# An encoder trunk whose weight chunks are split into a high and a low part by two DMA loads, in place of a load, a cast and a subtraction

## The chip, the cores and the metric

The kernel runs on one core of a Trainium2 chip. The metric is the device time of one execution in microseconds (us), median of several. The names of the engines in the profile: PE is TensorE (matmuls; PEld are its weight loads), DVE is VectorE, ACT is ScalarE, POOL is GpSimd, SP is SyncE, which here only issues DMAs (SPq is its queue).

## The reference

Two layers run over x, 512 tokens of width 1024, in float32. Each layer normalises x, projects it, runs two groups of heads (bidirectional retention and differential attention), adds their projection to x, and adds a gated feed-forward product:

```python
    for l in range(DEPTH):                      # DEPTH = 2
        h = rms_norm(x, attn_norm_g[l])
        proj = h @ w_in[l]
        rq, rk, rv, rg, dq, dk, dv = jnp.split(proj, split_at, axis=-1)
...
        ret = rms_norm(ret, ret_norm_g[l]) * jax.nn.silu(rg.reshape(shp))
...
        da = diff_attention(dqn, dkn, dv.reshape(B, S, DIFF_HEADS, DIFF_V_DIM), lam, slopes)
...
        x = x + jnp.concatenate([ret, da], axis=-1) @ w_out[l]

        h = rms_norm(x, ffn_norm_g[l])
        x = x + (jax.nn.silu(h @ w_gate[l]) * (h @ w_up[l])) @ w_down[l]
    return x
```

w_gate and w_up are 1024 x 2816 and w_down is 2816 x 1024, so more than half of the matmuls are in the feed-forward part.

## The kernel before

**Split products.** All weight products run on TensorE in the type fp32r, which keeps fewer bits than float32. To get float32's accuracy, each operand is split in two: a high part `hi`, the value rounded to fp32r, and a low part `lo`, the value minus `hi`. A product is then three matmuls, hi by hi, hi by lo and lo by hi (`mm3`, L173 to L176).

**Weight chunks.** Weights lie in HBM as chunks of 128 partitions by 1024 floats (512 KB; in the last pass over w_down 768 wide). `chunk` (L169) loads one into a tile `raw` (3 buffers) with a DMA that SP issues (L152), and splits it with `split_chunk`: ScalarE casts `raw` into `hi` (L166), and VectorE subtracts `hi` from `raw` into `lo` (L167). `hi` and `lo` have NHL = 3 buffers each. A full chunk feeds 24 matmuls of 512 columns (or as many operands of 256 columns for the value projections). There are 212 splits: 204 of chunks, and 8 half chunks at the start.

**Stages of a layer.** `project_first` (four weight chunks against all eight tiles of h), then values, gates and keys, the attention heads with further projections woven in between (`weave`), the retention pairs with the output projection woven in, the second norm, and the feed-forward part in three passes over 8, 8 and 6 tiles of the inner width (`FFN`): in each pass w_gate and w_up chunks in turn, then eight w_down chunks.

**The start.** In layer 0 the weights of `project_first` come as half chunks of 512 columns, `raw` and x by turns: for each of eight tiles x is loaded, split and scaled (`hi`, L185), squared (`sq`, L215) and summed. The constants `cst_sb` are loaded after all of it (L301). The eight short passes `wk` on ScalarE need them.

**What sets the order.** Code is written engine by engine through a framework that builds a graph, estimates each instruction's time and writes each engine's instructions in the order of that estimate. On the chip each engine, and the queue of DMAs that an engine issues, then works through its own list in order, and waits at an instruction until its semaphores are reached. Instructions of one engine do not overtake each other. Tiles come from pools: a new tile of a tag waits until the oldest buffer of the tag has been read for the last time.

Of the kernel before, what the change touches and what calls it, by code (L numbers as in the profile page):

```python
# [8 lines left out]
F32 = mybir.dt.float32  # L9
F32R = mybir.dt.float32r  # L10
AF = mybir.ActivationFunctionType
ALU = mybir.AluOpType

P = 128
# [21 lines left out]
PAIRS = [0, 0, 1, 0, 1, 2, 0, 1, 2, 3, 1, 2, 3, 2, 3, 3]  # L36


NW, NQK, NMIX, NAH, NHL = 12, 11, 20, 3, 3


PRM_AG, PRM_FG, PRM_RG, PRM_QG, PRM_KG, PRM_DG = 0, 16, 32, 34, 36, 38
# [9 lines left out]
def encoder_kernel(ctx: ExitStack, tc: tile.TileContext, xT, wfirst, wsingle, wvv, wout, wgu, wdn, prm, lam, cst, outT):  # L52
    nc = tc.nc
# [3 lines left out]
    wpool = ctx.enter_context(tc.tile_pool(name="wpool", bufs=3))  # L57
# [6 lines left out]
    def nm(s):  # L64
        uid[0] += 1
        return f"{s}{uid[0]}"

    def big(s, dt=F32, tag="w", bufs=NW):
        return tpool.tile([P, T], dt, tag=tag, name=nm(s), bufs=bufs)
# [19 lines left out]
    def f32(ap):  # L89
        return ap.bitcast(F32)  # L90
# [20 lines left out]
    xscr = ctx.enter_context(tc.tile_pool(name="dpool", bufs=1, space=bass.MemoryType.DRAM)).tile([KT, P, T], F32, name="xscr")  # L111

    def load_x(src, kt):
        xt = big("x", tag="qk", bufs=NQK)
        nc.sync.dma_start(xt, src[kt])
        return xt
# [26 lines left out]
    nc.vector.memset(eps_sb, EPS)  # L143


    def new_chunk(n, pieces=1):
        return wpool.tile([P, 1024], F32, tag="raw", name=nm("raw"), bufs=3), n, pieces

    def load_piece(new, src, i):
        raw, n, pieces = new  # L150
        s = slice(i * n // pieces, (i + 1) * n // pieces)
        nc.sync.dma_start(raw[:, s], src[:, s])  # L152

    def load_chunk(src, n=1024, pieces=1):
        new = new_chunk(n, pieces)
        for i in range(pieces):
            load_piece(new, src, i)
        return new

    def split_chunk(raw, n, pieces):  # L160
        hi = wpool.tile([P, 1024], F32R, tag="hi", name=nm("hi"), bufs=NHL)
        lo = wpool.tile([P, 1024], F32R, tag="lo", name=nm("lo"), bufs=NHL)
        q = n // pieces
        for i in range(pieces):
            s = slice(i * q, (i + 1) * q)
            nc.scalar.copy(hi[:, s], raw[:, s])  # L166
            nc.vector.tensor_tensor(lo[:, s], raw[:, s], f32(hi[:, s]), op=ALU.subtract)  # L167
        return hi, lo

    def chunk(*a, **kw):  # L170
        return split_chunk(*load_chunk(*a, **kw))

    def mm3(out, L, R, start, stop):  # L173
        nc.tensor.matmul(out, L[0], R[0], start=start, stop=False)  # L174
        nc.tensor.matmul(out, L[0], R[1], start=False, stop=False)  # L175
        nc.tensor.matmul(out, L[1], R[0], start=False, stop=stop)  # L176

    def cut(pair, *idx):
        return tuple(t[idx] for t in pair)

    def split_scaled(src, col, tag, bufs):

        hi = big("hi", F32R, tag, bufs)
        lo = big("lo", F32R, tag, bufs)
        nc.scalar.activation(hi, src, AF.Copy, scale=col)  # L185
        nc.vector.scalar_tensor_tensor(lo, src, col, f32(hi), op0=ALU.mult, op1=ALU.subtract)
        return hi, lo
# [88 lines left out]
        nc.vector.tensor_scalar(gk, prm_sb[:, PRM_KG : PRM_KG + DEPTH], -0.5, None, op0=ALU.mult)  # L276
        consts.update(gk=gk, lg=lg, lamn=lamn, gq=gq, gd=gd, wk=wk, rs=rs)

    def layer(l, n1, h, x_src, first_raw):


        def project_first():
            banks = [b() for b in (acc_bank, acc_bank, sc_bank, sc_bank)]
            for c in range(4):
                w = [t.rearrange("p (k f) -> p k f", f=512) for t in split_chunk(*first_raw[c])]
                for k in range(2):
                    kt = 2 * c + k
                    for i, ps in enumerate(banks):
                        mm3(ps, cut(w, slice(None), k, slice(i * P, (i + 1) * P)), h[kt], kt == 0, kt == KT - 1)
            return banks  # L290

        def project(name, m):
            w = [t.rearrange("p (k f) -> p k f", f=P) for t in chunk(wsingle[l, SINGLE.index((name, m))])]
            ps = acc_bank()
            for kt in range(KT):
                mm3(ps, cut(w, slice(None), kt), h[kt], kt == 0, kt == KT - 1)
            return ps

        first = project_first()
        if l == 0:  # L300
            nc.sync.dma_start(cst_sb, cst)  # L301
# [44 lines left out]
        def project_v(which, half, get=acc_bank):  # L346

            w = [[t.rearrange("p (k f) -> p k f", f=256) for t in chunk(wvv[l, which, half, i])] for i in range(2)]
            for i in range(4):
                ps = get()[:, :256]  # L350
                for kt in range(KT):
                    hh = cut(h[kt], slice(None), slice(i * P, (i + 1) * P))
                    mm3(ps, hh, cut(w[kt // 4], slice(None), kt % 4), kt == 0, kt == KT - 1)
                yield i, ps
# [190 lines left out]
        q, k = [None] * 4, [None] * 4  # L545
# [58 lines left out]
        def project_out(half, get, *then):  # L604
            parts = mix[4:] if half == 0 else mix[:4]
            for c in range(4):
                w = [t.rearrange("p (k f) -> p k f", f=256) for t in chunk(wout[l, half, c])]
                for m in (2 * c, 2 * c + 1):
                    if half == 0:
                        x.append(load_x(x_src, m))  # L610
                    ps = get()
                    for kt in range(4):
                        mm3(ps, cut(w, slice(None), kt, slice((m % 2) * P, (m % 2 + 1) * P)), parts[kt], kt == 0, kt == 3)
                    residual(m, x[m], ps, *then)
                    yield
# [13 lines left out]
        for a0, a1 in FFN:  # L629
            act = []  # L630
            for ff in range(a0, a1):
                pgu = []
                for gu in range(2):
                    w = [t.rearrange("p (k f) -> p k f", f=P) for t in chunk(wgu[l, ff, gu])]
# [12 lines left out]
            for m in range(KT):  # L647
                w = chunk(wdn[l, m][:, a0 * P : a1 * P], (a1 - a0) * P)
# [9 lines left out]
                        nc.sync.dma_start(outT[m], x[m])  # L658
        return n3, h3

    n, h, raws = Norm(), [], []
    for kt in range(KT):
        if kt % 2 == 0:
            raws.append(new_chunk(1024, 2))
        load_piece(raws[-1], wfirst[0, kt // 2], kt % 2)
        xt = load_x(xT, kt)
        h.append(split_scaled(xt, prm_sb[:, PRM_AG + kt : PRM_AG + kt + 1], "h", 16))
        n.add(xt)
    for l in range(DEPTH):
        if l:  # L670
            raws = [load_chunk(wfirst[l, c]) for c in range(4)]
        n, h = layer(l, n, h, xT if l == 0 else xscr, raws)


def _constants():
# [84 lines left out]
```

## Time and profile before

| | us |
|---|---|
| median of 3 runs | 1287.65 (1287.47 to 1289.41) |
| the profiled execution | 1287.41 |
| its span in the profile | 1285.6 |
| busy: TensorE, VectorE, ScalarE, GpSimd | 1271.1, 769.2, 570.5, 17.3 |
| load traffic | 93 GB/s mean |

How to read the profile's lines: a group has line, engine, operation, output tile <- input tiles, shapes and count, then busy us, mean ns of one, and the idle time of the engine ahead of it with what ended it. A timeline's line begins with start and duration in us. In a line of the waits stand the waiting engine, tile and line, the releaser, the total in us, the number and the longest. A table by stretches has the stretch, its length, busy us (and instructions) of PE, PEld, DVE, ACT and POOL, and then the granted TensorE clock, the DMA engines' busy share and GB/s. The matmuls' ends are modelled and overlap the next start, so the distance of starts says how fast TensorE goes.

The time of the profiled execution is 1.8 us longer than its span; the rest lies around it.

### The profile page before, as it was taken

The numbers are of one execution on the slowest core, as the hardware profiler recorded it, in microseconds if no ns is written. First come the engines' busy times: TensorE is split into PE (matmuls) and PEld (weight loads), VectorE is DVE, ScalarE is ACT, GpSimd is POOL, SyncE is SP. The second block draws the span as 40 slices with busy tenths as digits, with TensorE's granted clock in tenths as the row PEclk, the third lists the DMA queues.
The fourth block names the chain that finished last, engine by engine and source line by source line (L and its number), as shares of the span: only waits on it lengthen the run. The fifth ranks groups of instructions, "written<-read, shape, count | busy, mean of one in ns | idle before, by whom it ended". The sixth has DMA issues, their size and how long they took to land.

```text
span 1285.6 us, 15670 instructions
## 1 busy us (share of the span) xinstructions
PE 1271.1 (99%) x6192; PEld 1055.3 (82%) x6192; DVE 769.2 (60%) x1191; ACT 570.5 (44%) x887; POOL 17.3 (1%) x38
## 2 busy tenths in 40 slices
PE   8999999999999999999999999999999999999998
PEld 6888998678888888888888889977788888888887
DVE  6899759857443444344648997687664434443443
ACT  6777646544321222123438785564543223221221
POOL 1000000000000000000000000000000000000000
PEclk9999999999999999999999999999999999999999
DMA  7222224112333332332432122141233333333322
GB/s 263 82 67 66 67 66 148 36 64 98 99 94 103 99 98 82 114 91 85 160 109 83 50 83 66 56 141 50 66 101 96 98 98 98 98 98 98 93 80 90
DMA packets 36793, 120.07 MB, mean 93 GB/s; under 512 B 4208, under 2 KB 4208, under 8 KB 36592
## 3 DMA queue, kind: packets, MB, share of 16 engines
q1 hardware_dynamic: 36720, 119.08, 29.5%
q8 instruction: 48, 0.79, 0.3%
q14 instruction: 25, 0.20, 0.0%
HBM read 114.87 MB, written 4.19 MB: 93 GB/s over the span
## 4 chain that ended last, share of the span: by engine, by line
PE 97%; DVE 1%; ACT 1%; issue 0%; DMA 0%; SPq 0%
PE acc L174 15%; PE acc L175 14%; PE acc L176 14%; PE o L174 8%; PE o L176 8%; PE o L175 8%; PE sc L174 7%; PE sc L176 7%; PE sc L175 7%; PE sc L369 2%; PE o L469 2%; PE sc L454 1%; PE aux L385 1%; PE aux L128 1%; PE aux L129 1%; PE aux L430 1%
## 5 line engine op out<-in xcount | busy, mean ns | idle before, releaser
L166 ACT CAST hi<-raw 128x1024 fp32r<-128x1024 f32 (+2 forms) x212 | 215.7, 1019 | 510.0 <-issue 154.9
L174 PE MATMUL acc<-hi,hi 128*128 128x512 f32 (+1 forms) x914 | 337.3, 370 | 5.9 <-ACT hi L185 5.6
L175 PE MATMUL acc<-lo,hi 128*128 128x512 f32 (+1 forms) x914 | 338.3, 370 | 0.0
L176 PE MATMUL acc<-hi,lo 128*128 128x512 f32 (+1 forms) x914 | 337.7, 370 | 0.0
L167 DVE TENSOR_TENSOR lo<-raw,hi 128x1024 fp32r<-128x1024 f32 (+2 forms) x212 | 250.3, 1182 | 45.3 <-ACT hi L166 44.9
L174 PEld LDWEIGHTS acc<-hi,hi 128*128 128x128 f32 x914 | 172.6, 189 | 36.3 <-ACT hi L185 5.6
L175 PEld LDWEIGHTS acc<-lo,hi 128*128 128x128 f32 x914 | 172.5, 189 | 29.6 <-issue 1.2
L176 PEld LDWEIGHTS acc<-hi,lo 128*128 128x128 f32 x914 | 172.6, 189 | 29.2 <-issue 1.2
L174 PE MATMUL o<-hi,hi 128*128 128x512 f32 (+1 forms) x438 | 163.8, 374 | 2.2 <-DVE sq L481 2.2
L175 PE MATMUL o<-lo,hi 128*128 128x512 f32 (+1 forms) x438 | 163.6, 374 | 0.0
L176 PE MATMUL o<-hi,lo 128*128 128x512 f32 (+1 forms) x438 | 163.6, 374 | 0.0
L174 PE MATMUL sc<-hi,hi 128*128 128x512 f32 x408 | 159.4, 392 | 0.3 <-ACT hi L166 0.3
L176 PE MATMUL sc<-hi,lo 128*128 128x512 f32 x408 | 159.3, 390 | 0.0
L175 PE MATMUL sc<-lo,hi 128*128 128x512 f32 x408 | 159.2, 390 | 0.0
L174 PEld LDWEIGHTS o<-hi,hi 128*128 128x128 f32 x438 | 82.3, 188 | 17.6 <-DVE sq L481 2.7
L175 PEld LDWEIGHTS o<-lo,hi 128*128 128x128 f32 x438 | 82.4, 188 | 14.7
L176 PEld LDWEIGHTS o<-hi,lo 128*128 128x128 f32 x438 | 82.3, 188 | 14.6
L174 PEld LDWEIGHTS sc<-hi,hi 128*128 128x128 f32 x408 | 76.9, 189 | 18.6 <-issue 1.5
L176 PEld LDWEIGHTS sc<-hi,lo 128*128 128x128 f32 x408 | 76.9, 188 | 16.1
L175 PEld LDWEIGHTS sc<-lo,hi 128*128 128x128 f32 x408 | 76.9, 188 | 15.9
L103 ACT ACTIVATE sc<-sc,mx 128x512 f32<-128x512 f32 x64 | 46.0, 720 | 16.8 <-DVE mx L373 16.4
L599 DVE TENSOR_TENSOR x<-x,acc 128x512 f32<-128x512 f32 x36 | 24.6, 685 | 39.4 <-PE acc L176 39.3
(133 smaller groups left out, 1289.1 us busy)
## 6 DMA issues: line engine op xcount, KB each, us to landing
raw<-in_wgu SPq DMA_DIRECT2D x88, 512.0 KB, 3.5
raw<-in_wsingle SPq DMA_DIRECT2D x32, 512.0 KB, 3.5
raw<-in_wdn SPq DMA_DIRECT2D x32, 512.0 KB, 3.5
raw<-in_wvv SPq DMA_DIRECT2D x16, 512.0 KB, 3.5
raw<-in_wout SPq DMA_DIRECT2D x16, 512.0 KB, 3.6
raw<-in_wdn SPq DMA_DIRECT2D x16, 384.0 KB, 3.2
x<-in_xT SPq DMA_DIRECT2D x16, 256.0 KB, 4.2
raw<-in_wfirst SPq DMA_DIRECT2D x8, 256.0 KB, 5.2
```

The costliest lines, as they stand in the source:

```text
L103: i = nc.scalar.activation(out, src, f, **kw).ins
L128: nc.tensor.matmul(ps, w, hi, start=True, stop=False)
L129: nc.tensor.matmul(ps, w, lo, start=False, stop=True)
L166: nc.scalar.copy(hi[:, s], raw[:, s])
L167: nc.vector.tensor_tensor(lo[:, s], raw[:, s], f32(hi[:, s]), op=ALU.subtract)
L174: nc.tensor.matmul(out, L[0], R[0], start=start, stop=False)
L175: nc.tensor.matmul(out, L[0], R[1], start=False, stop=False)
L176: nc.tensor.matmul(out, L[1], R[0], start=False, stop=stop)
L369: nc.tensor.matmul(ps, q[m][:, t], k[m][part], start=part == 0, stop=part == 1)
L385: nc.tensor.transpose(tp[:, j * P : (j + 1) * P], a[:, j * P : (j + 1) * P], ident)
L469: nc.tensor.matmul(o[b, c * C : (c + 1) * C], v[pr // 2][2 * c + j][:, (pr % 2) * P + hh * HD : (pr % 2) * P + (hh + 1) * HD], s[c][:, hh, ...
L599: nc.vector.tensor_tensor(xt, xt, ps, op=ALU.add)
```

## The change

`chunk` no longer has a `raw` tile, a cast and a subtraction. GpSimd issues a DMA that loads the chunk from HBM straight into `hi`, which has the type fp32r, so that the DMA rounds. ScalarE writes minus `hi` into `lo` (a pass of the same shape as the cast was). GpSimd then issues a second DMA that loads the same chunk again and adds it to `lo` where it lies. NHL goes from 3 to 5 buffers, the three `raw` buffers go, and the tag `mix` has 18 tiles in place of 20. The eight half chunks of the start are still cast and subtracted (`split_piece`), from tiles of the tag `w`.

```diff
-NW, NQK, NMIX, NAH, NHL = 12, 11, 20, 3, 3
+NW, NQK, NMIX, NAH, NHL = 12, 11, 18, 3, 5
...
-    def split_chunk(raw, n, pieces):
-        hi = wpool.tile([P, 1024], F32R, tag="hi", name=nm("hi"), bufs=NHL)
-        lo = wpool.tile([P, 1024], F32R, tag="lo", name=nm("lo"), bufs=NHL)
-        q = n // pieces
-        for i in range(pieces):
-            s = slice(i * q, (i + 1) * q)
-            nc.scalar.copy(hi[:, s], raw[:, s])
-            nc.vector.tensor_tensor(lo[:, s], raw[:, s], f32(hi[:, s]), op=ALU.subtract)
+    def parts():
+        return [wpool.tile([P, 1024], F32R, tag=n, name=nm(n), bufs=NHL) for n in ("hi", "lo")]
+
+    def chunk(src, n=1024):
+
+        hi, lo = (t[:, :n] for t in parts())
+        nc.gpsimd.dma_start(hi, src)
+        nc.scalar.activation(lo, f32(hi), AF.Copy, scale=-1.0)
+        nc.gpsimd.dma_start(lo, src, accum_op=ALU.add)
         return hi, lo
 
-    def chunk(*a, **kw):
-        return split_chunk(*load_chunk(*a, **kw))
+    def split_piece(hi, lo, raw, s):
+        nc.scalar.copy(hi[:, s], raw)
+        nc.vector.tensor_tensor(lo[:, s], raw, f32(hi[:, s]), op=ALU.subtract)
...
-    n, h, raws = Norm(), [], []
+    n, h, early = Norm(), [], []
     for kt in range(KT):
         if kt % 2 == 0:
-            raws.append(new_chunk(1024, 2))
-        load_piece(raws[-1], wfirst[0, kt // 2], kt % 2)
+            early.append(parts())
+        s = slice(kt % 2 * 512, kt % 2 * 512 + 512)
+        raw = big("raw")
+        nc.sync.dma_start(raw, wfirst[0, kt // 2][:, s])
         xt = load_x(xT, kt)
+        split_piece(*early[-1], raw, s)
         h.append(split_scaled(xt, prm_sb[:, PRM_AG + kt : PRM_AG + kt + 1], "h", 16))
         n.add(xt)
     for l in range(DEPTH):
-        if l:
-            raws = [load_chunk(wfirst[l, c]) for c in range(4)]
-        n, h = layer(l, n, h, xT if l == 0 else xscr, raws)
+        first_w = (lambda c: chunk(wfirst[1, c])) if l else (lambda c: early[c])
+        n, h = layer(l, n, h, xT if l == 0 else xscr, first_w)
```

Since the framework orders each engine's list, the lists show more than the diff. In the brackets stand the semaphores that an instruction waits for: DMAHW are SP's loads, DMASW GpSimd's, the others an engine.

ScalarE at the start, before: cast of the weight piece, x's `hi` and its square come by turns, the third piece (`raw11`) after six passes.

```order
L166 CAST hi48_172<-raw1_78 128x512 [waits DMAHW1_49]
L185 ACTIVATE hi3_82<-x2_80,prm_sb_70 128x512 [waits DMAHW2_49]
L215 ACTIVATE sq5_86<-x2_80 128x512
L166 CAST hi48_172<-raw1_78 128x512 [waits DMAHW3_49]
L185 ACTIVATE hi7_91<-x6_89,prm_sb_70 128x512 [waits DMAHW4_49]
L215 ACTIVATE sq9_95<-x6_89 128x512
L166 CAST hi50_202<-raw11_99 128x512 [waits DMAHW5_49]
```

ScalarE after the change, from the third weight piece (`raw16`) to the sixth (`raw36`); 14 passes stand ahead of it, from the first piece's cast on.

```order
L158 CAST hi14_106<-raw16_108 128x512 [waits DMAHW3_49]
L203 ACTIVATE sq48_178<-x45_170 128x512 [waits DMAHW1_49,DVE_49]
L173 ACTIVATE hi46_174<-x45_170,prm_sb_70 128x512
L203 ACTIVATE sq54_192<-x51_184 128x512 [waits DMAHW2_49,DVE_49]
L173 ACTIVATE hi52_188<-x51_184,prm_sb_70 128x512
L103 ACTIVATE wk_350<-lg_316,cst_sb_72 128x8 [waits DMAHW4_49]
L103 ACTIVATE wk_350<-lg_316,cst_sb_72 128x8 x7
L158 CAST hi14_106<-raw22_122 128x512 [waits DMAHW5_49]
L180 CAST hi61_302<-ssum55_194 128x512 [waits DVE_49]
L158 CAST hi28_136<-raw30_138 128x512 [waits DMAHW6_49]
L158 CAST hi28_136<-raw36_152 128x512 [waits DMAHW7_49]
```

All eight tiles of x and the `wk` passes, which wait for the constants, now stand ahead of the cast of the fourth weight piece (`raw22`); before, `wk` stood behind all casts.

SP's loads at the start after the change, from the second to last tile of x to the seventh weight piece (`raw44`); the small parameters, six tiles of x and two weight pieces stand ahead of these rows:

```order
L115 DMA x45_170<-in_xT 128x512 [waits DMAHW1_49]
L115 DMA x51_184<-in_xT 128x512 [waits DMAHW2_49]
L655 DMA raw16_108<-in_wfirst 128x512 [waits DMAHW3_49]
L289 DMA cst_sb_72<-in_cst 128x2564 [waits DMAHW4_49]
L655 DMA raw22_122<-in_wfirst 128x512 [waits DMAHW5_49]
L655 DMA raw30_138<-in_wfirst 128x512 [waits DMAHW6_49]
L655 DMA raw36_152<-in_wfirst 128x512 [waits DMAHW7_49,DVE_49]
L655 DMA raw44_168<-in_wfirst 128x512 [waits DMAHW0_49,DVE_49]
```

The constants moved ahead of five weight pieces; before, they were the last of these loads.

GpSimd in the feed-forward part of layer 0, after the change, over five w_down chunks (before, GpSimd issued no load, and SP issued one `raw` load per chunk here):

```order
L152 DMA hi716_3515<-in_wdn 128x1024 [waits DMASW0_49,PE_49]
L152 DMA hi719_3546<-in_wdn 128x1024 [waits DMASW1_49,PE_49]
L154 DMA lo717_3516<-in_wdn 128x1024 [waits DMASW2_49,Activation_49]
L154 DMA lo720_3547<-in_wdn 128x1024 [waits DMASW3_49,Activation_49]
L152 DMA hi722_3577<-in_wdn 128x1024 [waits DMASW4_49,PE_49]
L154 DMA lo723_3578<-in_wdn 128x1024 [waits DMASW5_49,Activation_49]
L152 DMA hi725_3608<-in_wdn 128x1024 [waits DMASW6_49,PE_49]
L152 DMA hi728_3639<-in_wdn 128x1024 [waits DMASW7_49,PE_49]
L154 DMA lo726_3609<-in_wdn 128x1024 [waits DMASW0_49,Activation_49]
L154 DMA lo729_3640<-in_wdn 128x1024 [waits DMASW1_49,Activation_49]
```

All chunk loads moved from SP's list to GpSimd's, two for each chunk. The `hi` load waits for TensorE (its buffer is free when the chunk five before is used up), the `lo` load for ScalarE's pass. GpSimd's list holds 204 loads of each kind; SP's goes from 255 DMAs to 51.

More of the change, by code (lines that the diff above doesn't have):

```diff
@@ L143, in encoder_kernel @@
     nc.vector.memset(eps_sb, EPS)
[L146 to L155, printed above, removed]
-        for i in range(pieces):
-            load_piece(new, src, i)
-        return new
-    def split_chunk(raw, n, pieces):
-        hi = wpool.tile([P, 1024], F32R, tag="hi", name=nm("hi"), bufs=NHL)
-        lo = wpool.tile([P, 1024], F32R, tag="lo", name=nm("lo"), bufs=NHL)
-        q = n // pieces
-        for i in range(pieces):
-            s = slice(i * q, (i + 1) * q)
-            nc.scalar.copy(hi[:, s], raw[:, s])
-            nc.vector.tensor_tensor(lo[:, s], raw[:, s], f32(hi[:, s]), op=ALU.subtract)
+    def parts():
[5 more added lines that the diff above has]
+        nc.gpsimd.dma_start(lo, src, accum_op=ALU.add)
         return hi, lo
-    def chunk(*a, **kw):
-        return split_chunk(*load_chunk(*a, **kw))
+    def split_piece(hi, lo, raw, s):
+        nc.scalar.copy(hi[:, s], raw)
+        nc.vector.tensor_tensor(lo[:, s], raw, f32(hi[:, s]), op=ALU.subtract)
     def mm3(out, L, R, start, stop):
@@ L277, in prepare_small, with layer @@
         consts.update(gk=gk, lg=lg, lamn=lamn, gq=gq, gd=gd, wk=wk, rs=rs)
-    def layer(l, n1, h, x_src, first_raw):
+    def layer(l, n1, h, x_src, first_w):
         def project_first():
@@ L284, in project_first @@
             for c in range(4):
-                w = [t.rearrange("p (k f) -> p k f", f=512) for t in split_chunk(*first_raw[c])]
+                w = [t.rearrange("p (k f) -> p k f", f=512) for t in first_w(c)]
                 for k in range(2):
```

## The prediction

> **What bounds the kernel now.** I read the busy times first, then the chain that ended last, then the list of TensorE's waits.
>
> ```profile
> PE 1271.1 (99%) x6192; PEld 1055.3 (82%) x6192; DVE 769.2 (60%) x1191; ACT 570.5 (44%) x887; POOL 17.3 (1%) x38
> ...
> PE 97%; DVE 1%; ACT 1%; issue 0%; DMA 0%; SPq 0%
> ```
>
> TensorE (PE) is busy for 1271.1 of 1285.6 us, and 97% of the chain is its matmuls. VectorE (DVE), which the change relieves, is at 60%. What TensorE waits for, as total, times, longest:
>
> ```profile
> PE acc L174 <- ACT hi L185: 5.6, 1, 5.6
> PE o L174 <- DVE sq L481: 2.2, 1, 2.2
> PE sc L369 <- DVE mx L373: 1.9, 5, 0.5
> PE sc L174 <- ACT hi L166: 0.3, 1, 0.3
> PE acc L174 <- ACT hi L166: 0.3, 1, 0.3
> ```
>
> That is 10.3 us in all, of which 5.6 is the wait for the first operands. The last matmul ends at 1281.5, so 4.1 us more lie behind it. All idle time of TensorE is 14.5 us, and only the last two rows (0.6 us) wait for the weight split that is changed. A busy engine could still run slowly under load, so I look at how far apart matmuls start, once beside a full VectorE and once near the end (columns: start, duration):
>
> ```profile
> 22.06 0.39 PE L174 MATMUL acc<-hi,hi 128*128 128x512 f32 x1
> ...
> 24.78 0.39 PE L174 MATMUL acc<-hi,hi 128*128 128x512 f32 x1
> ```
>
> ```profile
> 1278.40 0.39 PE L176 MATMUL o<-hi,lo 128*128 128x512 f32 x1
> ...
> 1281.12 0.39 PE L176 MATMUL o<-hi,lo 128*128 128x512 f32 x1
> ```
>
> Twelve starts lie between the rows of each pair, 2.72 us both times: 0.227 us each, whatever VectorE does. Emptying VectorE cannot make matmuls faster. The gain is limited to waits; the loss is limited by nothing, since a chunk that comes late stops TensorE.
>
> **The change part by part.** What goes, and the loads as they are:
>
> ```profile
> L166 ACT CAST hi<-raw 128x1024 fp32r<-128x1024 f32 x188 | 197.7, 1053 | 466.7 <-issue 141.3 <-PE acc L175 124.8 <-PE sc L175 106.6
> ```
>
> ```profile
> L167 DVE TENSOR_TENSOR lo<-raw,hi 128x1024 fp32r<-128x1024 f32 x188 | 229.7, 1223 | 43.3 <-ACT hi L166 42.9
> ...
> L167 DVE TENSOR_TENSOR lo<-raw,hi 128x768 fp32r<-128x768 f32 x16 | 15.1, 956 | 0.0
> ```
>
> VectorE loses 229.7 + 15.1 = 244.8 us of work. It lay beside matmuls, so its own worth on the path is nothing, and next late is again TensorE. ScalarE (ACT) has as many passes as before, 204 negations for 204 casts, and I price one at the same 1.05 us. The two 0.3 us waits for L166 go with the path they were on: −0.6. The 1.9 and 2.2 us waits for VectorE could shrink too (0 to −4.1); I count nothing, since what would be late next there (ScalarE's exponent and casts) isn't moved out of the way.
>
> *The start.* The first eight half chunks are still split the old way, but in another order. The order of the changed kernel puts SP's constants ahead of the last five weight pieces, and ScalarE's eight wk passes, which wait for those constants, ahead of the cast of the fourth piece.
>
> ```profile
> 6.40 0.33 SPq L152 DMA_DIRECT2D raw<-in_wfirst  x1
> ...
> 10.47 0.33 SPq L301 DMA_DIRECT2D cst_sb<-in_cst  x1
> ```
>
> ```profile
> cst_sb<-in_cst SPq DMA_DIRECT2D x1, 1282.0 KB, 7.8
> ```
>
> ```profile
> 6.41 0.62 ACT L166 CAST hi<-raw 128x512 fp32r<-128x512 f32 x1 [0.35 <-DMA raw<-in_wfirst]
> ...
> 8.20 0.60 ACT L166 CAST hi<-raw 128x512 fp32r<-128x512 f32 x1
> ...
> 14.82 0.60 ACT L166 CAST hi<-raw 128x512 fp32r<-128x512 f32 x1
> ```
>
> ```profile
> 16.62 0.62 PE L174 MATMUL acc<-hi,hi 128*128 128x512 f32 x2
> ...
> 18.32 1.64 ACT L103 ACTIVATE wk<-lg,cst_sb 128x8 f32<-128x8 f32 x8
> ```
>
> From 6.40 to 10.47 SP issues a load each time that an earlier one has landed: six steps in 4.07 us, so a 256 KB load lands every 0.68 us. The third landed at 6.41. In the new order the third weight piece is the 11th load, at 6.41 + 8 × 0.68 = 11.9 us; the first 512 KB chunk that GpSimd now loads beside them may push it by two loads, to 13.2. The constants are five loads' worth: landed at 15.3 to 16.6. ScalarE's pace is (14.82 − 8.20)/12 = 0.55 us a pass. Eleven passes after 6.41 it reaches the third piece at 12.5 (or 13.2), five more passes bring it to wk at 15.3 to 16.0, wk starts with the constants at 15.3 to 16.6 and takes 1.64, and the fourth piece's cast, 0.6, is ready at 17.5 to 18.8. TensorE began its fourth group at 16.62 and now has to wait: a loss of **0.9 to 2.2 us**, of which I take the middle, 1.6. The other four pieces land by 20.0 and are cast at 0.55 us each, faster than the 2.72 us in which TensorE uses them. GpSimd's first chunk is not in question: its pass stands behind these casts, at about 22, and TensorE uses the product five groups, 13.6 us, after the gap.
>
> ```profile
> 9.59 0.63 PE L176 MATMUL sc<-hi,lo 128*128 128x512 f32 x1
> 10.02 0.63 PE L175 MATMUL sc<-lo,hi 128*128 128x512 f32 x1
> ```
>
> In this first group matmuls start 0.43 us apart, later 0.227. The Trainium skill ("TensorE: Matmul & The Clock Gate", Part 1: The HAM clock gate) has a rule for it: the array runs at half its clock until it has been busy for some 3.4 us, and falls back after an idle window as long. The rows agree that the start is slow, and still at 10.0, 4.4 us after the first matmul. By that rule my gap costs nothing more; had it grown past 3.4 us, some eight matmuls would take 0.2 us more each, an estimate of 1.6 us on top of the sum.
>
> *The chunk chain.* This is what decides. Before, SP issued one load per chunk and nothing hung on it. Now GpSimd (POOL) issues 408 loads, in order, and the accumulating one waits for a ScalarE pass that waits for the first to land; behind it stands the next chunk's load. In the feed-forward part its order goes hi, hi, lo, lo, hi, lo for chunks that share five buffers. A chunk is 24 matmuls, 5.44 us; five are 27.2. With g for one issue, L from issue to landing and A for the pass, a pair costs 2g + L + A (the first lo goes out while the second hi is under way) and a single g + L + A; five chunks are two pairs and a single: 5g + 3(L + A).
>
> ```profile
> L152 SPq DMA_DIRECT2D raw<-in_wgu x88: 327/328/328, 247.8 to 1218.9; - x88
> ...
> DMA to landing us min/median/max: 2.7/3.5/7.9
> ```
>
> ```profile
> 12.40 0.53 POOL L325 MEMSET klo<- 64x512 f32 x1 [9.48 <-DVE lo L186]
> ```
>
> No load from GpSimd, none that rounds and none that accumulates is in this trace. Bounds: g from SP's 0.33 to ScalarE's whole pass, 1.05; L from 3.5, the median, to 7.9, the slowest. Then five chunks take 1.65 + 3 × 4.55 = 15.3 us at least and 5.25 + 3 × 8.95 = 32.1 at most. I take the rows nearest in kind: GpSimd's own 0.53 and the median 3.5, 16.3 us, **hidden** with 10.9 to spare. The narrowest place is the last pass over w_down: eight 768-wide chunks at 18 × 0.227 = 4.08 us each, where the order is hi, lo one by one. A single must be through five times and land before TensorE, 38.1 us after the first buffer came free (four chunks of 5.44 and four of 4.08): 5(0.53 + L + 1.05) + L < 38.1, so L up to 5.0. At 3.5 it holds.
>
> One page of the Trainium skill speaks against moving loads to GpSimd ("SBUF — State Buffer", Who interferes with whom): GpSimd can't write a load's descriptors while VectorE runs in a mode that uses two ports, which TENSOR_SCALAR can enter. No load from GpSimd in this trace shows it either way; by the page the sum would be that of the third slower rival.
>
> *Buffers.* The tag mix has 18 tiles for 20. No row shows a wait for one; I bound a new one by the longest wait of TensorE after the start, 0 to 2.2, and take 0, the case of all rows but one.
>
> **The sum.** The profiled execution took 1287.41 us (span 1285.6): 1287.4 − 0.6 + 1.6 + 0 = **1288.4**, against the median of 1287.65.
>
> **Rivals.**
>
> *GpSimd's chain becomes the bound* (slower). It decides from L = 7.5 (g 0.33) or 6.3 (g 1.05) in the body, from 5.0 in the last pass. For it: a hi that is issued right behind a lo shares the engines with it, and the accumulating load must also read what it adds to. Against it: half the chain's time is spare at the median. At the upper end the feed-forward parts, 3168 matmuls × 0.227 = 718 us, grow by 32.1/27.2: +129, so 1417; if only the last passes are late, a few us.
>
> *The 16 DMA engines become the bound* (slower).
>
> ```profile
> 400.00:530.00 130.00, 130.00 (x575) 107.64 (x574) 55.62 (x64) 34.30 (x40) 0.00 (x0) 1.00 0.31 97
> ```
>
> Here a chunk takes 0.31 × 5.44 = 1.69 us of the engines (the columns before the last are granted clock and DMA share). Two plain loads are 3.4; with the accumulating one at two loads' worth 5.1, still under 5.44. From 2.2 loads' worth it binds; at three it would be 6.76 a chunk, +24% of 718 us: 1462.
>
> *VectorE's relief counts* (faster). The 1.9 and 2.2 us go as well: 1284.3. For it: L167 takes a third of VectorE's time. Against it: ScalarE stands in the same chains.
>
> *GpSimd is held up while VectorE scales the scores* (slower).
>
> ```profile
> L381 DVE TENSOR_SCALAR sc<-sc,c x32: 479/486/490, 67.3 to 813.5; 128x512 f32<-128x512 f32 x32
> ```
>
> 32 such operations of 0.49 us, all in the attention heads; if each held up a load that TensorE waits for, +15.6: 1304. Against it: a chunk there takes longer than 5.44 us, since TensorE has the heads' matmuls beside it, so the spare time is larger. This is the rule of the SBUF page named above, put into this kernel.
>
> *The loads don't round or don't subtract as said.* The kernel then computes something else in the same time; no separate price.
>
> **How the numbers follow.** A measurement of this kernel can tell about 0.2%, 2.6 us, from no change: 1285.1 to 1290.2. The hidden chain: 0.47, its own range 1285 to 1293 (relief and start, buffers); of it 0.32 within, 0.12 above, 0.03 below. GpSimd's chain 0.27, DMA engines 0.13, held up by VectorE 0.03, all slower. Relief 0.10: 0.08 faster, 0.02 same. Together 0.11 faster, 0.34 same, 0.55 slower. The range goes from 1283 (relief with the short start) to 1417 (the chain at its bound) and leaves out the DMA case and little else.
>
> **What would show it.** Right: no row of TensorE's waits names a DMA behind 40 us, landing from GpSimd under 5 us, one new gap of 1 to 2 us near 17. Wrong: waits of acc, sc or o for a DMA of lo or hi in the feed-forward parts, a DMA share near 1.0 there (engines) or well below it with GpSimd's issues late (chain); waits for VectorE gone (relief).

## The result and the profile after

The changed kernel takes 1447.67 us (median of 4 runs, 1444.73 to 1451.53), the kernel before 1287.56 in the same comparison: the ratio is 1.124, 95% interval 1.121 to 1.127. The forecast of 1288.4 was wrong; so was the range, whose upper end was 1417. The profile after, busy times and chain:

```profile
span 1443.0 us, 15849 instructions
PE 1324.9 (92%) x6192; PEld 1080.6 (75%) x6192; DVE 537.2 (37%) x987; ACT 563.3 (39%) x887; POOL 308.9 (21%) x446
...
issue 52%; PE 24%; POOL 13%; DMA 5%; ACT 4%; DVE 1%; POOLq 0%; SPq 0%; ACTq 0%
```

The change did to VectorE (DVE) what it says: 769.2 us became 537.2. But the chain is no longer TensorE's (PE 97% before, 24% now); 52% of it is `issue`, time for which the profile names nothing that was waited for. TensorE stands idle for 1443.0 − 1324.9 = 118.1 us (14.5 before), and it is busy for 53.8 us more with the same 6192 matmuls. No engine is full, so waits between engines are the bound; which ones, the rows below and the experiments tell. Where the time sits shows in the first and last silu pass (tile g) of the two feed-forward (FFN) parts, first before, then after (columns: duration min/median/max in ns, start of the first to start of the last):

```profile
L103 ACT ACTIVATE g<-g x22: 617/625/633, 308.7 to 607.4; 128x512 f32<-128x512 f32 x22
L103 ACT ACTIVATE g<-g x22: 616/625/633, 945.4 to 1244.2; 128x512 f32<-128x512 f32 x22
```

```profile
L103 ACT ACTIVATE g<-g x22: 612/615/634, 317.6 to 676.8; 128x512 f32<-128x512 f32 x22
L103 ACT ACTIVATE g<-g x22: 611/615/633, 1036.8 to 1397.5; 128x512 f32<-128x512 f32 x22
```

Between first and last silu pass, 298.7 and 298.8 us became 359.2 and 360.7: +122.4. The stretch up to the first one takes 8.9 us more, the one between the parts (338.0 to 360.0) 22.0, the tail 4.1. Together 157.4, the whole difference of the spans. A layer's last pass over w_down stands behind its last silu pass, so it is part of the 22.0 and of the 4.1: from the last silu pass to the last addition to x it took 37.4 and 37.3 us before (to 644.8 and 1281.5) and 46.3 and 41.5 after (to 723.1 and 1439.0), 13.1 more. So the FFN takes 122.4 + 13.1 = 135.5 of the 157.4.

The waits, first TensorE's largest, then GpSimd's (total, times, longest):

```profile
PE sc L164 <- DMA lo<-in_wgu: 18.5, 9, 3.2
PE acc L164 <- DMA lo<-in_wgu: 14.3, 8, 2.7
PE sc L162 <- ACT hi L180: 12.9, 3, 5.9
```

```profile
POOL lo L154 <- ACT lo L153: 882.5, 188, 9.2
POOL hi L152 <- PE acc L164: 116.0, 33, 8.9
```

TensorE waits for the accumulating load (`lo`), and for ScalarE's activation casts, which stand in ScalarE's list behind a negation that waits for a `hi` load (at 400.31 us a negation that ScalarE had waited 6.59 us to start, at 401.28 the cast behind it, at 401.93 TensorE). GpSimd itself spends 882.5 us, 61% of the span, in front of accumulating loads, waiting for the negation. It could have issued the next chunk's load in that time; its list holds that load back. Here is one round of three chunks in FFN 0 (layer 0's), GpSimd's rows (start, duration, idle before and what ended it):

```profile
472.74 0.88 POOL L152 DMA_DIRECT2D hi<-in_wgu  x1
481.56 0.86 POOL L154 DMA_DIRECT2D lo<-in_wgu  x1 [7.93 <-ACT lo L153]
482.10 1.45 POOL L152 DMA_DIRECT2D hi<-in_wgu  x2
489.84 0.89 POOL L154 DMA_DIRECT2D lo<-in_wgu  x1 [6.29 <-ACT lo L153]
491.31 0.87 POOL L154 DMA_DIRECT2D lo<-in_wgu  x1 [0.58 <-ACT lo L153]
491.85 0.88 POOL L152 DMA_DIRECT2D hi<-in_wgu  x1
```

A single and a pair, then the next single: 19.11 us for three chunks that TensorE could multiply in 3 × 5.44 = 16.32. The two long waits in brackets, 7.93 + 6.29, each for a landing and the negation behind it, are 14.2 of it. Landing times from issue (last column, medians):

```profile
hi<-in_wgu POOLq DMA_DIRECT2D x88, 512.0 KB, 6.9
lo<-in_wgu POOLq DMA_DIRECT2D x88, 512.0 KB, 5.6
```

### The profile page after: what moved, and what is told of

The parts are those of the page before. It is cut to its first block, busy times and chain, and to the rows that moved or that the text cites. A ratio compares the mean times of both kernels' runs of the same rounds, so it can differ in the third digit from the quotient of the medians.

```text
span 1443.0 us, 15849 instructions
## 1 busy us (share of the span) xinstructions
PE 1324.9 (92%) x6192; PEld 1080.6 (75%) x6192; DVE 537.2 (37%) x987; ACT 563.3 (39%) x887; POOL 308.9 (21%) x446
## 3 DMA queue, kind: packets, MB, share of 16 engines
q0 software_dynamic: 58752, 209.74, 63.5%
## 4 chain that ended last, share of the span: by engine, by line
issue 52%; PE 24%; POOL 13%; DMA 5%; ACT 4%; DVE 1%; POOLq 0%; SPq 0%; ACTq 0%
POOL hi L152 7%; POOL lo L154 6%; PE acc L164 4%; PE acc L162 4%; PE acc L163 4%; DMA hi<-in_wsingle 2%; PE o L457 1%; PE sc L164 1%; PE sc L162 1%; PE sc L163 1%; PE sc L442 1%; PE o L164 1%; PE o L163 1%; PE o L162 1%; ACT lo L153 1%
## 5 line engine op out<-in xcount | busy, mean ns | idle before, releaser
L153 ACT ACTIVATE lo<-hi 128x1024 fp32r<-128x1024 f32 (+1 forms) x204 | 212.2, 1041 | 741.2 <-DMA hi<-in_wgu 337.0
L162 PE MATMUL acc<-hi,hi 128*128 128x512 f32 (+1 forms) x914 | 345.5, 378 | 20.8 <-ACT rv L492 6.1
L164 PE MATMUL acc<-hi,lo 128*128 128x512 f32 (+1 forms) x914 | 344.1, 377 | 21.1 <-DMA lo<-in_wgu 14.3
L163 PE MATMUL acc<-lo,hi 128*128 128x512 f32 (+1 forms) x914 | 343.2, 376 | 0.2 <-DVE lo L181 0.2
L164 PE MATMUL sc<-hi,lo 128*128 128x512 f32 x408 | 165.2, 406 | 24.9 <-DMA lo<-in_wgu 18.5
L164 PE MATMUL o<-hi,lo 128*128 128x512 f32 (+1 forms) x438 | 168.8, 385 | 9.0 <-DMA lo<-in_wdn 7.2
L162 PE MATMUL sc<-hi,hi 128*128 128x512 f32 x408 | 163.8, 402 | 12.9 <-ACT hi L180 12.9
L154 POOL DMA_DIRECT2D lo<-in_wgu x88 | 76.7, 875 | 404.5 <-ACT lo L153 389.5
L181 DVE TENSOR_TENSOR lo<-u,hi 128x512 fp32r<-128x512 f32 x44 | 30.5, 692 | 220.8 <-ACT hi L180 220.6
L632 DVE TENSOR_TENSOR u<-g,u 128x512 f32<-128x512 f32 x44 | 30.4, 692 | 164.7 <-ACT g L103 164.0
```

The lines of the kernel that those rows point to most:

```text
L153: nc.scalar.activation(lo, f32(hi), AF.Copy, scale=-1.0)
L154: nc.gpsimd.dma_start(lo, src, accum_op=ALU.add)
L181: nc.vector.tensor_tensor(lo, src, f32(hi), op=ALU.subtract)
L632: nc.vector.tensor_tensor(u, g, u, op=ALU.mult)
```

## The experiments

Two theories stood against each other. **Chain**: GpSimd's in-order list waits out a landing L and a negation A for each single or pair of chunks. With g for one issue, the round above costs 3g + 2(L + A) = 3 × 0.88 + 2 × (6.9 + 1.05) = 18.5 us, where the rows show 19.11. **Engines**: the rounding and the accumulating load of a chunk keep the 16 DMA engines for longer than its 5.44 us. All edits are to the changed kernel's function `chunk`, unless another place is named; `order` is a dependency that only fixes the order within one engine's list.

| run | what differs | us | TensorE's clock | GpSimd's queue, share of 16 engines |
|---|---|---|---|---|
| before | | 1287 | 1.00 | |
| after | | 1447.7 | 0.964 | 63.5% |
| e1 | rounding load two chunks ahead | 1311.9 | 0.992 | 73.7% |
| e2 | rounding load one chunk ahead | 1293.7 | 0.997 | 74.5% |
| e3 | second load plain | 1295.0 | 0.996 | 52.8% |
| e4 | no negation, second load plain | 1277.6 | 1.00 | 51.1% |
| e5 | strictly in turn | 1765.1 | 0.928 | 53.5% |
| e6 | e2, negation on VectorE | 1287.5 | 0.997 | 75.2% |
| e7 | accumulating load alone | 1363.8 | 0.981 | 46.4% |
| e8 | e2, negation partly on GpSimd | 1297.7 | 0.995 | 74.4% |
| e9 | e6, start in the old order | 1289.4 | 0.997 | 74.8% |

e1, e6, e8 and e9 were timed in several runs; e2, e3, e4, e5 and e7 are single ones.

**e1 and e2: the order alone.**

```diff
-        nc.gpsimd.dma_start(hi, src)
+        load = nc.gpsimd.dma_start(hi, src).ins
+        if len(added) >= 2:
+            tc.add_manual_dep(added[-2], load.name, order, reason="issue order")
...
-        nc.gpsimd.dma_start(lo, src, accum_op=ALU.add)
+        added.append(nc.gpsimd.dma_start(lo, src, accum_op=ALU.add).ins)
```

That is e1; e2 has 1 and `added[-1]` in place of 2 and `added[-2]`.

> Same loads, same arithmetic, same bytes; only the order of GpSimd's list differs: the rounding load of a chunk is issued two chunks ahead of the accumulating one. Chain theory (GpSimd's in-order list waits out each landing: 3 g + 2 (L + A) = 3 x 0.88 + 2 x (6.9 + 1.05) = 18.5 us for three chunks against 16.3 of matmuls): here a landing is waited out once in three chunks, (2 x 0.88 + 6.9 + 1.05) / 3 = 3.2 us a chunk, below 5.44, so 1288 to 1300 us, no wait of TensorE for a lo DMA in the FFN, DMA share there about 0.8. Engine theory (rounding plus accumulating load of a chunk keep the 16 DMA engines for longer than 5.44 us): bytes and loads are the same, so 1430 to 1460 us and the waits for lo stay.

> As before, but the rounding load is issued only one chunk ahead of the accumulating one. Chain theory: a landing is waited out once in two chunks, (2 x 0.88 + 6.9 + 1.05) / 2 = 4.9 us a chunk, still below 5.44: 1288 to 1310 us, with small waits for lo where a landing is later than 8 us. Engine theory: 1430 to 1460 us.

e1 took 1311.92 us (ratio to the kernel before 1.018, 1.016 to 1.020), e2 1293.73. One reordering takes away 154 of 160 us, and the loads, bytes and passes are the same 408, 209.74 MB and 204. The stretch 450 to 600 us in the table by stretches, after and e2 (PE, PEld, DVE, ACT and POOL busy, then granted clock, DMA share, GB/s):

```profile
450.00:600.00 150.00, 137.17 (x564) 110.14 (x563) 26.35 (x40) 33.35 (x40) 34.41 (x48) 0.94 0.69 160
```

```profile
450.00:600.00 150.00, 150.00 (x664) 124.20 (x663) 33.16 (x48) 41.09 (x48) 39.57 (x56) 1.00 0.90 193
```

664 matmuls in place of 564, TensorE without a gap, and the engines *busier*, at 0.90. They weren't full in the changed kernel; they were waiting for GpSimd. That settles it against the engine theory. e1's time missed its expectation by 12 us. The chain of GpSimd is gone there too, but its first row of waits shows what came instead:

```profile
POOL hi L154 <- PE acc L168: 501.7, 92, 15.5
```

The `hi` load two chunks ahead waits for its buffer, and the accumulating load that is due stands behind it. e1 waits like that 92 + 49 + 46 times, and TensorE then waits for `lo` at the edges of stages (3.2 us at one place for `lo<-in_wout`). That this is the whole of e1's 18 us over e2 is argued from the rows, not tried separately.

**e3 and e4: the accumulation and the negation left out.**

```diff
-        nc.gpsimd.dma_start(lo, src, accum_op=ALU.add)
+        nc.gpsimd.dma_start(lo, src)
```

That is e3; e4 also takes out the negation.

> The second load of a chunk is a plain load of the same bytes: the addition onto minus the high part is left out, the negation and every wait stay. Chain theory, if a landing takes as long behind plain loads: unchanged, 1430 to 1450 us; if the rounding load's 6.9 us come from accumulating loads ahead of it in the queue, its landing falls towards the 3.7 us seen at the least, 3 x 0.88 + 2 x (3.7 + 1.05) = 12.1 us for three chunks, below 16.3, so 1290 to 1310 us. Engine theory: an accumulating load would be the dear one, the engines' share falls well under 0.70 in the FFN and the time to about 1290.

> Negation and addition are left out: two loads a chunk, one rounding and one plain, neither waiting for the other. Chain theory: nothing is left to wait for in GpSimd's list but buffers; 2 x 0.88 = 1.76 us a chunk; 1287 to 1295 us, with ScalarE's waits for hi loads gone and PE's clock at 0.99. Engine theory with a dear rounding load: still over 1400 us.

e3 took 1294.96 us with every wait and the list order of the chain still there. Its landings and GpSimd's rows:

```profile
hi<-in_wgu POOLq DMA_DIRECT2D x88, 512.0 KB, 4.7
lo<-in_wgu POOLq DMA_DIRECT2D x88, 512.0 KB, 3.9
```

```profile
L152 POOL DMA_DIRECT2D hi<-in_wgu x88: 527/535/548, 263.7 to 1230.6; - x88
```

Behind plain loads, `hi` lands in 4.7 us where it took 6.9, and an issue takes 0.53 us where it took 0.88: 3 × 0.53 + 2 × (4.7 + 1.05) = 13.1 us for three chunks, below 16.32. So the changed kernel's L is not that of a load that rounds; it is that of a load behind one that accumulates. e4, 1277.6 us with `hi` at 3.8 us, shows what is left without negations: TensorE's idle time is 12.5 us there, and it is 9 us faster than the kernel before. That is about what a free negation and a free addition could be worth; it is one run, and its products lack a part.

**e5: the same loads strictly in turn.**

```diff
+        if added:
+            tc.add_manual_dep(load, added[-1].name, order, reason="issue order")
```

> The other way round from e1 and e2: GpSimd's list holds the two loads of each chunk strictly in turn, rounding, accumulating, rounding, accumulating; the same loads, bytes and buffers. Chain theory: a chunk costs 2 g + L + A = 2 x 0.88 + (5.0 to 6.4) + 1.05 = 7.8 to 9.2 us against 5.44 of matmuls, over the FFN's 132 chunks 310 to 500 us more than before: 1600 to 1780 us, ScalarE's wait for the hi load ended by GpSimd in every chunk. Engine theory: the loads ask the engines for no more than in the changed kernel, so 1430 to 1460 us.

1765.09 us, inside what the chain theory gave (1600 to 1780) and over 300 us above what the engine theory gave. GpSimd, one chunk:

```profile
488.35 0.88 POOL L154 DMA_DIRECT2D hi<-in_wdn  x1
496.00 0.86 POOL L158 DMA_DIRECT2D lo<-in_wdn  x1 [6.77 <-ACT lo L157]
496.55 0.88 POOL L154 DMA_DIRECT2D hi<-in_wdn  x1
```

8.20 us a chunk, of which 6.77 is GpSimd's wait for the landing and the pass. The time of this kernel follows from the order of one list: 1765 in turn, 1448 in singles and pairs, 1294 one ahead.

**e7: the price of an accumulating load.** The raw chunk comes by a plain load of SP, ScalarE rounds and negates it, and GpSimd issues accumulating loads only (three pairs of buffers in place of five, three for the raw chunk, 20 tiles in the tag mix).

```diff
+        raw = wpool.tile([P, 1024], F32, tag="raw", name=nm("raw"), bufs=3)[:, :n]
...
-        nc.gpsimd.dma_start(hi, src)
+        nc.sync.dma_start(raw, src)
+        nc.scalar.copy(hi, raw)
```

> The accumulating load measured without the rounding one: the raw weights come by SP's plain loads, ScalarE rounds and negates them, and GpSimd issues only the 204 accumulating loads; three pairs of buffers and three raw ones in place of five pairs. Both theories: an accumulating load keeps the 16 engines for about 3.1 us (the 1.67 of a plain one and the 1.40 by which e1's queue is dearer than e3's per load), so GpSimd's queue at 204 x 3.1 = 630 us, 48 to 49% of the span, and a landing of 4 to 6 us. Chain theory: GpSimd's list holds no landing that another load must wait for, so 1285 to 1315 us; ScalarE at some 780 us may cost a part of it.

```profile
q0 software_dynamic: 29376, 104.87, 46.4%
```

0.464 × 1362.0 / 204 = 3.10 us of the 16 engines for one accumulating load. For the loads of e4, of which none accumulates, it is 0.511 × 1275.8 / 408 = 1.60. So accumulating costs 1.9 plain loads, and a chunk 3.10 + 1.60 = 4.7 us of 5.44. The time, 1363.8, missed the expectation of 1285 to 1315: FFN 0 runs at full pace from 450 to 600 us (661 matmuls), but waits of 2 to 7.6 us stand in other stages. Fewer buffers and two ScalarE passes per chunk differ at once here; which of them it is stays open.

**e6, e8 and e9: can the repaired kernel beat the one before?** e6 is e2 with the negation on VectorE, e8 with the negation of the 68 chunks outside the FFN on GpSimd (the expectation counts 72), e9 is e6 with SP's start in the old order.

```diff
-        negs.append(nc.scalar.activation(lo, f32(hi), AF.Copy, scale=-1.0).ins)
+        negs.append(nc.vector.tensor_scalar(lo, f32(hi), -1.0, None, op0=ALU.mult).ins)
```

> e2 with the negation moved from ScalarE to VectorE, which is at 42% in e2 (60% before the change). Chain theory with ScalarE as what was left in the attention stages: between e4 (1277.6, no negation at all) and e2 (1293.7), so 1280 to 1290 us, ScalarE's busy time near 372 us. If the few waits left are those for VectorE (L361 for DVE mx, L228 for DVE rstd): 1293 to 1300 us, longer than e2.

> e2 with the negation of the 72 chunks outside the FFN moved from ScalarE to GpSimd itself, where it stands between the next chunk's rounding load and the accumulating one; in the FFN it stays on ScalarE. If ScalarE's 1.04 us negations in the attention stages were what e4 gained (1277.6 against e2's 1293.7): 1278 to 1286 us, ScalarE near 450 us busy. If a negation on GpSimd lasts several us, the chain there becomes (2 x 0.88 + 6.2 + A) / 2 a chunk, over the 7.9 us a chunk of those stages (570 us for 72 chunks) from A = 7.8 us: then slower than e2, 1295 us or more.

> e6 with SP's first sixteen loads (pieces of the first weights and of x) put back in turn, as they stand before the change, and the constants behind them; in e6 five loads of x went ahead of the second piece of weights and TensorE stood 2.67 us at 12.75 us, with some seven matmuls at half pace (0.2 us each) behind the gap. If that gap goes: 2.7 + 1.4 = 4 us less than e6, 1283 to 1285 us, 0.2 to 0.3% under the kernel before. If the rounding loads of GpSimd are what delays the pieces: the gap stays, 1286 to 1289 us.

e6 took 1287.51 us, ratio 1.0008 (0.9997 to 1.0018): no difference to the kernel before, though VectorE has 105 us and ScalarE 199 us less to do than there. It is 6 us under e2's one time, as expected if ScalarE's negations were what was left. e8 took 1297.66 (1.008, 1.007 to 1.010), 4 us more than e2's one time. A negation on GpSimd takes 2.87 us:

```profile
L162 POOL TENSOR_SCALAR lo<-hi 128x1024 fp32r<-128x1024 f32 x68 | 195.4, 2874 | 15.1 <-DMA hi<-in_wfirst 6.7 <-DMA hi<-in_wvv 3.9 <-DMA hi<-in_wsingle 2.7
```

That is below the 7.8 us from which the expectation made it bind, so neither of its two cases came true; ScalarE was busy for 508 us, not for 450. TensorE's longest new wait is one of 3.5 us for `lo<-in_wfirst`. VectorE was busy for 21 us more than in e2 (563.9 against 542.7): its scaling of the scores, for one, e2 and then e8:

```profile
L373 DVE TENSOR_SCALAR sc<-sc,c 128x512 f32<-128x512 f32 x32 | 15.5, 486 | 1.0
L378 DVE TENSOR_SCALAR sc<-sc,c 128x512 f32<-128x512 f32 x32 | 20.7, 648 | 0.9
```

That VectorE slows down beside GpSimd's negations may be the rest of the 4 us over e2; no run tries it alone. In e9 the start gap went as expected (54 matmuls in the first 20 us, 37 in e6), but the time did not: 1289.42 us, ratio 1.002 (1.0005 to 1.003). Other gaps stand in its profile, one of 2.28 us at 70.88 among them. No version that computes the whole product beats the kernel before.

## Why the prediction was wrong

*The chunk chain* is the step that failed: "the median 3.5, 16.3 us, **hidden** with 10.9 to spare". The mechanism had been written down, as the first rival, with the right place; in the sum, L was mis-sized. The sign that the prediction set for it came: waits for `lo` in the FFN at a DMA share well below 1.0 (0.69), with GpSimd's issues late. L was taken from SP's plain loads, mostly one in flight at a time (3.5). In the changed kernel `hi` is issued right behind a load that keeps the engines for 3.1 us, and lands in 6.9. In the sum of three chunks that is 2 × 3.4 = 6.8 us, and g, 0.88 in place of 0.53, adds 1.05 (at the most: in the round above the next issue starts 0.54 us behind one, at 481.56 and 482.10, so these durations overlap). Plain second loads (e3) gave 4.7 and 0.53, and the chain was hidden as forecast: of the 3.4 us that L was short, 2.2 come with the addition, and 1.2 stay without it. The reason stood in the text ("shares the engines with it, and the accumulating load must also read what it adds to"), and it was weighed as a chance of 0.27, not put into L.

*The pattern* failed with it: "five chunks are two pairs and a single". In the FFN, up to its last passes, the order is mostly a single and a pair by turns, so two landings are waited out for three chunks, not three for five. By the prediction's own sum for five chunks, the measured g and L give 5 × 0.88 + 3 × 7.95 = 28.3 us against 27.2, 4% over; for three chunks the same values give 18.5 against 16.3, 14% over. The chain of three binds from L = (16.32 − 2.64)/2 − 1.05 = 5.8, not from 6.3 to 7.5.

*The upper end of the range*, 1417, was the chain at L = 7.9 in the FFN with everything else free: +129. With two landings for three chunks the FFN came to +135.5, at a lower L. Of this the last passes over w_down, rightly named the narrowest place (L up to 5.0; `hi` landed there in 5.6), have 13.1. The other 21.9 us lie in front of the FFN parts, for which the sum had nothing but the 1.6 of the start.

*The clock*: the step cited the Trainium skill ("TensorE: Matmul & The Clock Gate", Part 1: The HAM clock gate) for a fall to half clock after an idle window of some 3.4 us, and let shorter gaps cost nothing more. TensorE's rows of the changed kernel (start, duration):

```profile
473.47 0.39 PE L163 MATMUL acc<-lo,hi 128*128 128x512 f32 x1
476.08 0.50 PE L164 MATMUL acc<-hi,lo 128*128 128x512 f32 x1 [2.22 <-DMA lo<-in_wgu]
...
477.06 0.63 PE L164 MATMUL acc<-hi,lo 128*128 128x512 f32 x1
477.48 0.63 PE L162 MATMUL acc<-hi,hi 128*128 128x512 f32 x1
...
480.53 0.40 PE L164 MATMUL acc<-hi,lo 128*128 128x512 f32 x1
480.76 0.39 PE L162 MATMUL acc<-hi,hi 128*128 128x512 f32 x1
```

After a gap of 2.22 us, matmuls start 0.43 us apart from 476.65 to 480.04, then 0.23 again. The trace doesn't agree with 3.4 us as the gap that it takes; the price, some eight matmuls at 0.2 us more, is the 1.6 us estimated there. Over the whole span the granted clock was 0.964, and 0.036 × 1443.0 = 52 us is nearly all of the 53.8 for which TensorE is busy longer. How much of it adds to the time is not shown: where GpSimd's list sets the pace, TensorE might have waited instead.

*The engines as the bound* were rightly put second: "From 2.2 loads' worth it binds". e7 and e4 give 1.9, and e2 runs at full pace with a share of 0.90. The margin is small.

*VectorE's relief* was rightly counted at nothing. In e2 VectorE is at 542.7 us and TensorE still waits 3.1 us for its `mx`.

*GpSimd held up while VectorE scales the scores* left no mark: four of GpSimd's issues ran beside such an operation and took 0.54 to 0.92 us, the others 0.53 to 1.21. Outside the chain, GpSimd's accumulating loads were late with no releaser shown in two cases, 9.2 us together.

*The start* lay at the upper end of what was worked, "a loss of **0.9 to 2.2 us**", but only in part for the reason given. The fourth group of matmuls, at 16.62 before, starts here:

```profile
18.82 0.50 PE L162 MATMUL acc<-hi,hi 128*128 128x512 f32 x1 [1.29 <-ACT hi L158]
```

It is 2.2 us later, and 1.29 is the gap that was worked out: the fourth piece's cast, behind wk. Another gap, of 1.36 us at 11.71, was not foreseen: TensorE waits for the second piece's cast, which ScalarE runs at 11.06, behind eight passes over x. e9, with the old order, has neither. *Buffers* of the tag mix show in no row of TensorE's waits.

## What to carry to other kernels

Where a load waits for a pass that waits for another load of the same issuing engine, count the round trip on that engine's list, not the engine's busy time (21% here): issue the next chunk's independent load ahead of the waiting one; here one chunk ahead did better than two (1293.7 against 1311.9, with five pairs of buffers). Take the landing time for such a sum from loads under the load that the change will make; a single plain load's median was a lower bound here (3.5 against 6.9). Take the repeating pattern from the list over many chunks, not from one stretch of five. And ask first what the relieved engine was worth: VectorE, 226 us lighter in e2, gave nothing.

## What the runs showed of the hardware

An accumulating load of 512 KB took 3.10 us of the 16 DMA engines where a plain or rounding one took 1.60 (the mean of both kinds), and its issue 0.87 us on GpSimd where theirs took 0.53 (e7, e4). A rounding load issued right behind an accumulating one also showed 0.88 us, but it started 0.55 us behind it (e5, 496.00 and 496.55), so the two overlap.

TensorE's clock fell after gaps shorter than the forecast had it. In TensorE's rows of the changed kernel from 40 us on, of 16 gaps of 0.8 to 1.64 us none was followed by matmuls at half pace (0.43 us apart, or 0.21 with 256 columns), of 25 gaps of 2.1 us and more 23 were. It is no sharp threshold: gaps of 2.37 and 3.19 us, at 1197.45 and 1352.04, were not. So behind a wait of 2 us and more TensorE mostly lost another 1.6 us of work.

A VectorE negation of 128x1024 lasted 0.695 us (e6, mean of 188), against 1.22 for the subtraction before; on GpSimd one took 2.87, and VectorE's 32 scalings of the scores rose from 486 to 648 ns in that run (e8 against e2).
